# Windowed-attention scores from split queries and keys, saved to DRAM by the projection blocks

## The chip, the cores and the metric

One core of one Trainium2 chip runs the whole program. The metric is the device time of one execution in microseconds (us), the median of several. The core's engines are TensorE (PE, matrix products; its weight loads are listed as PEld), VectorE (DVE), ScalarE (ACT), GpSimd (POOL) and SyncE (SP, which here only issues DMAs). Each works through its own instruction list in order.

## The reference: what is computed

One layer of a hybrid trunk on 1024 tokens of 1024 channels. A normed input is multiplied by `w_in`; the columns go to three groups of heads, the joined outputs are multiplied by `w_out` and added; then follow a gated MLP with a short convolution, a gated per-layer embedding and a last norm. The change touches group B, the mixture of dilated attention windows (4 heads of width 64):

```python
for window, dil in SW_PATTERNS:        # (128, 1), (512, 4), (2048, 16)
    o, lse = banded_causal_attention(stride_gather(q, dil), stride_gather(k, dil),
                                     stride_gather(v, dil), window // dil)
    ...
wts = jax.nn.softmax(jnp.stack(lses, 0), axis=0)
o = jnp.sum(wts[..., None] * jnp.stack(outs, 0), axis=0)
```

The kernel forms it as one masked softmax over all keys up to the query, with the logarithm of how many windows hold a key added to its score. Group A is HGRN2 (4 heads of 128), group C is RWKV-7.

## The kernel before, in words

**Products in two kinds.** Dense products are made from split operands: a value's high part (type fp32r, the cast on line 104 or 152) and the rest (the subtraction on line 106 or 154); high by high, high by rest and rest by high are three fp32r products (`mm3`, lines 122 to 131). Products on raw fp32 operands, the attention scores among them, show as two records in the trace for each product in the program.

**The mixing phase** (`phase_mix`, line 301) has two stages. In the first, `rwkv` alternates the two head pairs of group C with projections of 128 columns, numbered by the list on line 492 and grouped by `FILL` on line 508. A projection block (`project_rest`, line 419) makes 48 products into a PSUM tile `dp`, evicts it on DVE or ACT into an SBUF tile `zst` (two buffers) and stores that to a DRAM tile z*j* on SP's queue (line 433). Blocks 24, 25, 26 are queries, keys and values of the first head pair of group B, 27, 28, 29 those of the second; 8 to 23 are the four blocks (f, q, v, gate) of each HGRN head. The last block made in this stage is 27. Four are left: 28, 29, 19, 23.

In the second stage (line 310) four generators take turns in a list written on lines 318 to 321: A (HGRN heads 0 and 2), B (heads 1 and 3), C (`swa`, the attention), F (`project_late`, the four blocks left, whose PSUM tiles are named `zp`). A scheduler then sets each engine's list from this program. Stream C loads q, k and v of a pair on POOL's queue (`swa_load`, line 1033; four buffers of the tag `sslot`), and for each of 8 blocks of 128 queries makes scores (`swa_scores`, line 1052), adds mask and takes the row extreme (line 1070, DVE), exponentiates (line 1072, ACT), transposes (line 1086) and multiplies by the values (line 1099). The score products on line 1063 use 64 rows of the array for each head. HGRN heads take their tiles from a pool of 11 (`slot`).

**The outputs** of the eight groups of 128 channels stay in SBUF (`self.o`). `o_split` (line 1117) splits one into the operands of the `w_out` product when those operands (`self.O`) exist; until then it notes it in `done`, and the end of `project_late` (lines 465 to 467) splits what is noted. As F's end is reached in the program after all other streams, all eight are noted; the scheduler moves each split to where its operands and buffers are ready. `phase_out` (line 1124) then multiplies: `rows(m)` takes the groups in the order 6, 7, 0, 1, 4, 2, 3, 5, the first two row blocks for both halves of the tokens.

The one-time load of masks, `ctmp` (line 281, POOL's queue), is placed in the pool `pre0` that opens with group C.

Of the kernel before, what the change touches and what calls it, by code (L numbers as in the profile page):

```python
# [18 lines left out]
P = 128  # L19
# [60 lines left out]
class Trunk:  # L80
# [220 lines left out]
    def phase_mix(self):  # L301
        nc, tc = self.nc, self.tc
        self.mix_norm()
# [115 lines left out]
    def project_rest(self, js, hooks={}):  # L419
# [3 lines left out]
        for j in js:  # L423
# [6 lines left out]
            for part in parts:  # L430
                self.finish(kind, *part)
            d = self.zpool.tile([P, T], F32, tag=f"z{j}", name=f"z{j}")
            nc.sync.dma_start(d, t)
            self.z[j] = d

# [9 lines left out]
    def project_late(self, js):  # L445
# [19 lines left out]
        self.O = self.xall()  # L465
        for k in self.done:
            self.o_split(k)

# [16 lines left out]
    def rwkv(self):  # L485
# [194 lines left out]
    def rwkv_norm(self, p, sg, d, hf):  # L680
# [9 lines left out]
        if hf == 0:  # L690
            d["o"] = self.keep.tile([P, T], F32, tag="oc", name=self.nm("oc"), bufs=2)
        o = d["o"][:, sl]
# [19 lines left out]
        if hf:  # L712
            self.o[6 + p] = d["o"]
            self.dump(f"o{6 + p}", d["o"])

    def dump(self, name, t):
# [316 lines left out]
    def swa_load(self, sp, p):  # L1033
        d = {"p": p}
        for i, n in enumerate("qkv"):
            d[n] = self.zload(24 + 3 * p + i, lambda n: sp.tile([P, T], F32, tag="sslot", name=self.nm(n), bufs=4),
                              self.nc.gpsimd)
        return d

    def swa_values_in(self, d):  # L1040
        nc, vc = self.nc, d["v"]
        V = self.sp.tile([P, T], F32, tag="sslot", name=self.nm("sV"), bufs=4)
        for hf in (0, 1):
            pt = self.mxp.tile([P, HT], F32, tag="mx", name=self.nm("vt"))
            for c in range(4):
                nc.tensor.transpose(pt[:, c * P:(c + 1) * P], vc[:, hf * HT + c * P:hf * HT + (c + 1) * P], self.ident)
            nc.scalar.copy(V[:, hf * HT:(hf + 1) * HT], pt)
        d["V"] = V.rearrange("p (b c) -> p b c", c=P)

    HEADS = slice(0, 64), slice(64, 128)  # L1050

    def swa_scores(self, sp, d, qb):
# [7 lines left out]
        for b in range(0, nk, HT):  # L1060
            w = min(HT, nk - b)
            for h, hs in enumerate(self.HEADS):
                nc.tensor.matmul(pq[h][:, b:b + w], d["q"][hs, qb * P:nk], d["k"][hs, b:b + w], start=True, stop=True)
        lgs = []
# [590 lines left out]
```

## Time and profile before

| what | us |
|---|---|
| median of 3 executions | 1521.87 |
| lowest and highest | 1519.84 and 1521.97 |
| the profiled execution | 1520.86 |
| its span, first to last instruction | 1519.0 |
| mean granted TensorE clock in it | 0.986 of full speed |
| PE busy | 1468.0 |
| DVE busy | 1087.5 |
| ACT busy | 634.8 |
| POOL busy | 431.6 |

The profile is one execution. Its times count from the start of the span. A row of its timeline gives start, length, engine, line, operation, output and inputs, and in brackets how long the engine stood idle before it and what ended that. Matmuls overlap in the pipeline, so their lengths add up to more than the time that they take; the distance from start to start is the better price.

### The profile page before, as it was taken

Reading aid. Unit: us, or ns where it says so; the run is one execution under the profiler, and the core shown is the slowest. Engines: PE = TensorE matmul, PEld = TensorE weight load, DVE = VectorE, ACT = ScalarE, POOL = GpSimd, SP = SyncE. Lnnn points to the kernel's source line nnn. Section 1 sums busy time; section 2 is a strip of 40 time slices with the busy share of each in tenths; the row PEclk is TensorE's granted clock in tenths of the full one; section 3 lists DMA queues with packets and bytes.
Section 4 is the critical chain, followed back from the end, with each engine's and each line's share of the span. In section 5 each row is a group of like instructions: output and inputs, shape, how many; then the busy total and the mean of one; then the engine's idle time right before and its main releaser. Section 6 shows DMA issues by size and latency. Waiting matters only on the chain. (4 is left out here: it accounts for less than half of the span.)

```text
span 1519.0 us, 20098 instructions
## 1 busy us (share of the span) xinstructions
PE 1468.0 (97%) x7452; PEld 1213.5 (80%) x7452; DVE 1087.5 (72%) x1574; ACT 634.8 (42%) x1091; POOL 431.6 (28%) x360
## 2 busy tenths in 40 slices
PE   8999999999999899999999999999999999999995
PEld 7888887888877686778778888888888888888774
DVE  7666443674456578745888888888888799767684
ACT  6533322323324545425454444444444444455541
POOL 2234221315222132113124444444444000003330
PEclk9999999999999999999999999999999999999998
DMA  6124002123052121166333333333333873451352
GB/s 216 56 90 125 15 29 84 56 90 84 1 214 64 70 70 56 43 216 200 111 111 104 104 104 104 105 104 105 104 104 109 308 276 99 123 145 52 109 182 75
DMA packets 78865, 167.82 MB, mean 110 GB/s; under 512 B 19952, under 2 KB 20080, under 8 KB 78768
## 3 DMA queue, kind: packets, MB, share of 16 engines
q1 hardware_dynamic: 64992, 145.44, 29.3%
q10 hardware_dynamic: 12688, 17.04, 3.4%
q0 software_dynamic: 1088, 4.06, 0.8%
q8 instruction: 58, 0.95, 0.3%
q14 instruction: 39, 0.32, 0.1%
HBM read 120.12 MB, written 46.40 MB: 110 GB/s over the span
## 5 line engine op out<-in xcount | busy, mean ns | idle before, releaser
L127 PE MATMUL dp<-xh,whi 128*128 128x512 f32 x544 | 185.7, 399 | 1.4 <-ACT xh L367 1.4
L129 PE MATMUL dp<-xl,whi 128*128 128x512 f32 x544 | 182.8, 393 | 0.4 <-DVE xl L368 0.3
L131 PE MATMUL dp<-xh,wlo 128*128 128x512 f32 x544 | 182.0, 393 | 0.5 <-DVE wlo L106 0.5
L106 POOL TENSOR_TENSOR wlo<-wraw,whi 128x512 fp32r<-128x512 f32 x59 | 80.1, 1358 | 270.7 <-ACT whi L104 266.1
L106 POOL TENSOR_TENSOR wlo<-raw,whi 128x512 fp32r<-128x512 f32 x84 | 134.8, 1623 | 76.2 <-ACT whi L104 76.2
L104 ACT CAST whi<-wraw 128x512 fp32r<-128x512 f32 x120 | 73.1, 618 | 167.6 <-PE dp L129 120.4
L1210 PE MATMUL bg<-t,whi 128*128 128x512 f32 x352 | 133.2, 389 | 0.0
L127 PEld LDWEIGHTS dp<-xh,whi 128*128 128x128 f32 x544 | 100.8, 188 | 24.3 <-issue 3.3
L131 PEld LDWEIGHTS dp<-xh,wlo 128*128 128x128 f32 x544 | 101.8, 188 | 22.1 <-DVE wlo L106 1.3
L129 PEld LDWEIGHTS dp<-xl,whi 128*128 128x128 f32 x544 | 101.6, 188 | 22.2 <-DVE xl L368 1.2
L106 POOL TENSOR_TENSOR wlo<-s,whi 128x512 fp32r<-128x512 f32 x44 | 64.2, 1459 | 172.2 <-ACT whi L104 172.2
L1501 PE MATMUL bg<-t,whi 128*128 128x512 f32 x308 | 95.2, 390 | 0.0
L1501 PE MATMUL bv<-t,whi 128*128 128x512 f32 x308 | 94.9, 389 | 0.0
L104 ACT CAST whi<-raw 128x512 fp32r<-128x512 f32 x88 | 52.7, 620 | 94.9 <-issue 48.5
L104 ACT CAST whi<-s 128x512 fp32r<-128x512 f32 x66 | 38.9, 620 | 122.0 <-PE bg L1210 113.3
L106 DVE TENSOR_TENSOR wlo<-wraw,whi 128x512 fp32r<-128x512 f32 x61 | 50.7, 831 | 43.5 <-ACT whi L104 40.1
L1210 PEld LDWEIGHTS bg<-t,whi 128*128 128x128 f32 x352 | 66.1, 188 | 13.8
L168 POOL TENSOR_TENSOR rst<-rst,mhalf 128x4 f32<-128x4 f32 x8 | 9.8, 1226 | 230.6 <-DVE rst L166 230.6
L1501 PEld LDWEIGHTS bv<-t,whi 128*128 128x128 f32 x308 | 57.8, 188 | 12.0
L1501 PEld LDWEIGHTS bg<-t,whi 128*128 128x128 f32 x308 | 57.8, 188 | 11.8
L1210 PE MATMUL bg<-t,wlo 128*128 128x512 f32 x176 | 67.2, 389 | 0.0
L1497 ACT CAST t<-t 128x512 fp32r<-128x512 f32 x77 | 47.8, 622 | 44.4 <-PE bv L1501 30.3
(406 smaller groups left out, 3702.4 us busy)
## 6 DMA issues: line engine op xcount, KB each, us to landing
raw<-in_ffn_up_dram SPq DMA_DIRECT2D x44, 512.0 KB, 3.7
wraw<-in_w_in_dram SPq DMA_DIRECT2D x29, 512.0 KB, 3.7
z<-zst SPq DMA_DIRECT2D x18, 512.0 KB, 3.1
gb<-ct SPq DMA_DIRECT2D x33, 256.0 KB, 2.0
t<-gb SPq DMA_DIRECT2D x33, 256.0 KB, 2.8
t<-gt SPq DMA_DIRECT2D x33, 256.0 KB, 2.7
zl<-z SPq DMA_DIRECT2D x16, 512.0 KB, 3.5
wraw<-in_ple_gate_dram SPq DMA_DIRECT2D x16, 512.0 KB, 3.7
```

The lines of the kernel that those rows point to most:

```text
L104: nc.scalar.copy(hi, src)
L106: eng.tensor_tensor(lo, src, hi.bitcast(F32), ALU.subtract)
L127: nc.tensor.matmul(ps[hf], wh, xh[hf], start=first, stop=False)
L129: nc.tensor.matmul(ps[hf], wh, xl[hf], start=False, stop=False)
L131: nc.tensor.matmul(ps[hf], wl, xh[hf], start=False, stop=last)
L168: nc.gpsimd.tensor_tensor(r2, r, self.mhalf[:, :4], ALU.pow)
L1210: nc.tensor.matmul(ps, w[part == 2][:, s], X[k][part == 1], start=start and k == part == 0, stop=k == 3 and part == 2, skip_group_check=no ...
L1497: nc.scalar.copy(xh, x)
L1501: nc.tensor.matmul(ps[m], wt[part == 2][:, m * P:(m + 1) * P], (xh, xl)[part == 1], start=k == part == 0, stop=k == NK - 1 and part == 2)
```

## The change

The projection blocks 24, 25, 27 and 28 (queries and keys) are evicted as before, then split: an ACT copy makes the fp32r high part `zhi` (another `zst` buffer), a DVE subtraction leaves the rest in place, and both are stored. For each query block four small loads build two stationary tiles `qs`: the high part of one head's queries on its 64 rows, their rest on the other 64. The keys' high part of each head is loaded twice, on both halves of the rows (`kh`), the rest once (`kl`). A score is then one product over 128 rows (high and rest of the queries by the keys' high part) and one over 64 rows (high by rest), both fp32r, where it was one fp32 product over 64 rows.

What goes with it: all loads of the attention are issued on SP's queue; block 27 and 28 trade places with 22, so that 28 is the last block before the second stage and 29, 22, 19, 23 are left; every output is stored to DRAM by `o_split` and loaded again at the end of `project_late`; the outputs of group C move from the pool that lives through the phase to the first stage's pool; HGRN's pool has 10 tiles.

```diff
-        self.O, self.done = None, []
-        for p in (0, 1):
-            self.o_split(6 + p)
...
-            self.slots, self.NSLOT = slots, 11
+            self.slots, self.NSLOT = slots, 10
...
+            if j in (24, 25, 27, 28):
+                hi = self.keep.tile([P, T], F32R, tag="zst", name=self.nm("zhi"), bufs=2)
+                nc.scalar.copy(hi, t)
+                nc.vector.tensor_tensor(t.bitcast(F32R), t, hi.bitcast(F32), ALU.subtract)
+                self.zsave(f"h{j}", hi.bitcast(F32))
+                self.zsave(f"l{j}", t)
+            else:
+                self.zsave(j, t)
...
         for k in self.done:
+            self.o[k] = self.zload(f"o{k}", self.slot)
             self.o_split(k)
...
-        js = iter((*range(8, 16), 24, 25, 26, 16, 17, 18, 20, 21, 22, 27, 28, 29, 19, 23))
+        js = iter((*range(8, 16), 24, 25, 26, 16, 17, 18, 20, 21, 27, 28, 29, 22, 19, 23))
...
+        for h in (0, 1):
+            t = sp.tile([P, T], F32R, tag="kk", name=self.nm("kh"), bufs=5)
+            for q in self.HEADS:
+                nc.sync.dma_start(t[q].bitcast(F32), self.z[f"h{j + 1}"][self.HEADS[h]])
+            d["kh"].append(t)
+        d["kl"] = sp.tile([P, T], F32R, tag="kk", name=self.nm("kl"), bufs=5)
+        nc.sync.dma_start(d["kl"].bitcast(F32), self.z[f"l{j + 1}"])
+        d["qs"] = self.swa_queries(sp, d, 0)
+        d["v"] = self.zload(j + 2, lambda n: sp.tile([P, T], F32, tag="lg", name=self.nm(n), bufs=4))
...
+    def swa_queries(self, sp, d, qb):
+        qs = []
+        for h in (0, 1):
+            t = sp.tile([P, P], F32R, tag="qs", name=self.nm("qs"), bufs=4)
+            for i in (0, 1):
+                self.nc.sync.dma_start(t[self.HEADS[h ^ i]].bitcast(F32), d["z"][i][self.HEADS[h], qb * P:(qb + 1) * P])
+            qs.append(t)
+        return qs
...
+            for h in (0, 1):
+                nc.tensor.matmul(pq[h][:, b:b + w], d["qs"][h], d["kh"][h][:, b:b + w], start=True, stop=False)
             for h, hs in enumerate(self.HEADS):
-                nc.tensor.matmul(pq[h][:, b:b + w], d["q"][hs, qb * P:nk], d["k"][hs, b:b + w], start=True, stop=True)
+                nc.tensor.matmul(pq[h][:, b:b + w], d["qs"][h][hs], d["kl"][hs, b:b + w], start=False, stop=True)
+        if qb < 7:
+            d["qs"] = self.swa_queries(sp, d, qb + 1)
...
     def o_split(self, k):
         if self.O is None:
+            self.zsave(f"o{k}", self.o[k])
             self.done.append(k)
             return
```

The change also reorders each engine's list. On SP, where the second stage begins, stand in the kernel before the load of the last projection weights, the store of block 22, the first four HGRN loads (z8, z9 of head 0; z12, z13 of head 1) and only then the store of the last block, 27:

```order
L95 DMA wraw_855_4423<-in_w_in_dram 128x1024
L433 DMA z22_3522<-zst_660_3519 128x1024
L471 DMA zl_678_3633<-z8_801 128x1024
L471 DMA zl_679_3635<-z9_973 128x1024
L471 DMA zl_749_3904<-z12_1168 128x1024
L471 DMA zl_750_3906<-z13_1236 128x1024
L433 DMA z27_3606<-zst_674_3604 128x1024
```

At the same place of SP's list in the changed kernel stand the rest of block 28's split (zl28; its high part is the row ahead), the keys' rest kl, the four loads of the first query block, the values, and z8 and z9 of HGRN head 0:

```order
L441 DMA zl28_3629<-zst_677_3622 128x1024
L1053 DMA kl_681_3656<-zl25_2092 128x1024
L1063 DMA qs_682_3658<-zh24_1999 64x128
L1063 DMA qs_682_3658<-zl24_2001 64x128
L1063 DMA qs_683_3661<-zh24_1999 64x128
L1063 DMA qs_683_3661<-zl24_2001 64x128
L479 DMA zl_684_3664<-z26_2466 128x1024
L479 DMA zl_685_3666<-z8_801 128x1024
L479 DMA zl_686_3668<-z9_973 128x1024
```

So the first loads of the second stage moved from ahead of the last block's store to behind it. On PE, in the kernel before, products of `phase_out` (dp, operands xh and xl) stand among the last of HGRN head 3 and the attention; these are the first of them:

```order
L1086 MATMUL swt_1020_5151<-cst_76,lg_993_5016 128x128 x4
L127 MATMUL dp_1100_5501<-xh_1089_5403,whi_1098_5497 128x512
L1086 MATMUL swt_1021_5157<-cst_76,lg_993_5016 128x128 x3
L919 MATMUL hsc_1026_5172<-qt_948_4828,ks_1010_5109 128x128 x4
L127 MATMUL dp_1100_5501<-xh_1073_5387,whi_1098_5497 128x512
L129 MATMUL dp_1100_5501<-xl_1090_5404,whi_1098_5497 128x512
```

In the changed kernel the first product of `phase_out` on PE follows the last transposes of HGRN head 3 (vt from ho):

```order
L991 MATMUL hpo_1091_5519<-hV_1080_5463,hS_995_5033 128x128
L1011 MATMUL vt_1097_5548<-cst_76,ho_1090_5518 128x128 x4
L1011 MATMUL vt_1098_5554<-cst_76,ho_1090_5518 128x128 x4
L127 MATMUL dp_1146_5704<-xh_1127_5590,whi_1144_5700 128x512
L127 MATMUL dp_1146_5704<-xh_1111_5574,whi_1144_5700 128x512
L129 MATMUL dp_1146_5704<-xl_1128_5591,whi_1144_5700 128x512
```

The 35 products that stood ahead of those transposes moved behind them.

More of the change, by code (lines that the diff above doesn't have):

```diff
@@ L302, in phase_mix @@
         nc, tc = self.nc, self.tc
+        self.O, self.done = None, []
         self.mix_norm()
@@ L431, in project_rest, with zsave @@
                 self.finish(kind, *part)
-            d = self.zpool.tile([P, T], F32, tag=f"z{j}", name=f"z{j}")
-            nc.sync.dma_start(d, t)
-            self.z[j] = d
+            if j in (24, 25, 27, 28):
[6 more added lines that the diff above has]
+                self.zsave(j, t)
+    def zsave(self, j, t):
+        self.z[j] = self.zpool.tile([P, T], F32, tag=f"z{j}", name=f"z{j}")
+        self.nc.sync.dma_start(self.z[j], t)
     def finish(self, kind, dst, src, r):
@@ L690, in rwkv_norm @@
         if hf == 0:
-            d["o"] = self.keep.tile([P, T], F32, tag="oc", name=self.nm("oc"), bufs=2)
+            d["o"] = self.slots.tile([P, T], F32, tag="oc", name=self.nm("oc"), bufs=2)
         o = d["o"][:, sl]
@@ L714, in rwkv_norm @@
             self.dump(f"o{6 + p}", d["o"])
+            self.o_split(6 + p)
     def dump(self, name, t):
@@ L1033, in swa_load @@
     def swa_load(self, sp, p):
[L1034 to L1037, printed above, removed]
-        return d
+        nc, d = self.nc, {"p": p}
+        j = 24 + 3 * p
+        d["z"] = self.z[f"h{j}"], self.z[f"l{j}"]
+        d["kh"] = []
+        for h in (0, 1):
[7 more added lines that the diff above has]
+        d["v"] = self.zload(j + 2, lambda n: sp.tile([P, T], F32, tag="lg", name=self.nm(n), bufs=4))
+        return d
+    def swa_queries(self, sp, d, qb):
[6 more added lines that the diff above has]
+        return qs
     def swa_values_in(self, d):
         nc, vc = self.nc, d["v"]
-        V = self.sp.tile([P, T], F32, tag="sslot", name=self.nm("sV"), bufs=4)
+        V = self.sp.tile([P, T], F32, tag="sV", name=self.nm("sV"), bufs=1)
         for hf in (0, 1):
```

## The prediction

> **What bounds the kernel now.** I read the page first (busy shares, the span in 40 slices), then busy time by windows, then the timeline around each place that the change touches.
>
> ```profile
> PE 1468.0 (97%) x7452; PEld 1213.5 (80%) x7452; DVE 1087.5 (72%) x1574; ACT 634.8 (42%) x1091; POOL 431.6 (28%) x360
> PE   8999999999999899999999999999999999999995
> DVE  7666443674456578745888888888888799767684
> PEclk9999999999999999999999999999999999999998
> 480.00:520.00 40.00, 40.00 (x255) 31.16 (x256) 24.12 (x44) 19.27 (x36) 6.08 (x5) 1.00 0.08 27
> 520.00:560.00 40.00, 32.92 (x239) 28.15 (x236) 24.62 (x44) 19.65 (x37) 8.43 (x8) 0.87 0.30 106
> 560.00:600.00 40.00, 36.41 (x259) 29.12 (x258) 33.58 (x63) 22.44 (x47) 14.24 (x12) 0.96 0.23 73
> 600.00:620.00 20.00, 18.95 (x153) 14.22 (x152) 18.84 (x40) 12.01 (x24) 3.87 (x3) 1.00 0.08 27
> ```
>
> The last four rows are windows; behind start, end and length stand the busy times of PE, PEld, DVE, ACT and POOL, the granted clock, the DMA share and GB/s. PE sets the pace nearly everywhere. The attention runs from 445 to 644 us. Until 520 PE is never idle; from 520 to 560 it lacks 7 us and runs at 0.87 of its clock; from 560 to 620 DVE is busy 52.4 of 60 us and PE still 55.4. So a microsecond saved on PE counts fully in the first half of this stage and partly in the second, and a wait at the head of PE's list there moves everything behind it.
>
> **The scores themselves.** The timeline of PE gives the price of a burst by the distance to the next row:
>
> ```profile
> 455.00 0.70 PE L1063 MATMUL swq<-zl,zl 64*128 64x256 f32 x4
> 455.63 0.44 PE L1086 MATMUL swt<-cst,lg 128*128 128x128 f32 x2
> 462.80 0.92 PE L1063 MATMUL swq<-zl,zl 64*128 64x384 f32 x4
> 463.64 0.44 PE L1099 MATMUL swo<-pT,sV 128*64 128x128 f32 x4
> 519.52 1.13 PE L1063 MATMUL swq<-zl,zl 64*128 64x512 f32 x4
> 520.58 1.53 PE L1099 MATMUL swo<-pT,sV 128*64 128x128 f32 x24
> 513.88 0.47 PE L127 MATMUL zp<-xh,whi 128*128 128x512 f32 x1
> 519.21 0.39 PE L131 MATMUL zp<-xh,wlo 128*128 128x512 f32 x1
> 453.12 1.95 PE L898 MATMUL hsc<-zl,hk 128*128 128x128 f32 x16
> ```
>
> A burst is two heads by two records. It takes 0.63, 0.84 and 1.06 us for 256, 384 and 512 keys: 0.2 us fixed and 0.21 for each 128 keys. The two heads therefore share the array: the time is that of two records, not four. A burst of 128 keys is then 0.42. The code has 12 bursts of 512 (blocks 3, 4, 5 and 6 once and block 7 twice, for each of two pairs) and 4 each of 384, 256 and 128: 12.7 + 3.4 + 2.5 + 1.7 = 20.3 us, a little more where the heads stand apart.
>
> The fp32r products of a projection follow each other every 0.23 us (the first and last of 24 above, (519.21 - 513.88) / 23). The new burst has two such products over 128 rows and two over 64 rows. If the latter overlap as the old ones do, a burst of 512 costs 3 x 0.23 + 0.2 = 0.89; if not, 1.12. Scaled by width, with 0.12 us as least step of a small product (1.95 / 16), 384, 256 and 128 cost 0.72, 0.56 and 0.56, or 0.89, 0.68 and 0.68. The sum is 18.0 us or 22.4. So what can be gained in products is small: 2.3 us at best by this sum, where heads stand apart before perhaps 5, or a loss of 2. I take a gain of 3, range -2 to 6.
>
> The fixed 0.2 us is weighed once more, since it falls on each change between 128-row and 64-row products, and the new code changes in and out in each of 24 bursts, the old one only in each of 16 blocks. The Trainium skill, "TensorEngine Tiling (Array Packing)", section "Key Properties", says that changing the tiling mode drains TensorE. By that rule the 0.2 us is a price of every change, as counted above; without it the new sum would be 4.8 us lower.
>
> **The start of the stage.** These rows show what PE, DVE and SP did there, and the usual landing times (issues, KB, median us to landing, within 440 to 660 or 40 to 440 us):
>
> ```profile
> 434.89 3.07 SPq L471 DMA_DIRECT2D zl<-z  x4
> 441.13 0.81 DVE L877 TENSOR_SCALAR zl<-zl,olb,lb 128x1024 f32<-128x1024 f32 x1 [5.52 <-DMA zl<-z]
> 443.63 0.62 PE L131 MATMUL dp<-xh,wlo 128*128 128x512 f32 x2
> 445.06 0.48 PE L1063 MATMUL swq<-zl,zl 64*128 64x128 f32 x2
> 446.08 1.22 DVE L438 TENSOR_TENSOR zst<-dp,rstd 128x1024 f32<-128x1024 f32 x1
> zl<-z SPq DMA_DIRECT2D x12, 512.0 KB, 3.3
> z<-zst SPq DMA_DIRECT2D x17, 512.0 KB, 3.1
> At<-scz SPq DMA_DIRECT2D x4, 64.0 KB, 3.1
> L441 ACT ACTIVATE zst<-dp x18: 594/600/1028, 91.7 to 425.7; 128x512 f32<-128x512 f32 x16, 128x1024 f32<-128x1024 f32 x2
> ```
>
> Before, the HGRN loads were issued from 434.9, nine microseconds ahead of the last product of block 27 (443.9), and PE went on with scores at 445.06. In the changed list kl, the first qs, the values, z8 and z9 stand behind both stores of block 28. That block ends on PE at the same 443.9; then DVE evicts (1.2, to 445.3), ACT copies 1024 elements (1.0, to 446.5), DVE subtracts (1.2, to 447.8), SP issues the store, kl and four qs (6 x 0.33, to 449.9), and loads land 3.1 to 3.3 us after their issue: kl at 451.7, the last qs near 452.5, the values at 453.4, z8 and z9 near 454. PE's next rows are the scores, then the transposes of the values, then the products of F, so it waits from 443.9 to about 452.5, where it lost about 1.4 before: 7 us more.
>
> A long wait has a second price, seen at 528 us:
>
> ```profile
> 528.74 0.80 PE L1063 MATMUL swq<-zl,zl 64*128 64x128 f32 x4 [4.01 <-DMA zl<-z]
> 528.70:535.00 6.30, 5.91 (x25) 5.00 (x26) 1.05 (x6) 0.88 (x4) 0.00 (x0) 0.50 0.09 36
> ```
>
> After 4.01 us of idleness PE had half its clock for 6.3 us, which lost about 3 us of work. Eight idle microseconds bring at least that: +3. The start of the stage costs 10 us (range 4 to 14: less if HGRN, whose loads come 13 us late, can catch up; more if the loads, 3 MB with the two stores, queue behind each other).
>
> **The middle.** The same 4.01 us vanish in turn: they were the load of the second pair's queries and keys, which needed the four `sslot` buffers of the first. Now kh has five buffers, its second pair is loaded early, and between the last read of the first kh and the first need of the second kl PE's list holds transposes, HGRN products and 24 products of F, over 6 us against a landing time of 3.3. The gain is 4 us and the 3 of the clock: -7 (range -8 to -3, if another late load takes its place).
>
> **The end of the stage.** The products of `phase_out` that filled PE's waits stand behind HGRN head 3 now:
>
> ```profile
> 627.02 0.48 PE L127 MATMUL dp<-xh,whi 128*128 128x512 f32 x1
> 654.69 0.39 PE L131 MATMUL dp<-xh,wlo 128*128 128x512 f32 x1
> 656.87 1.06 PE L1002 MATMUL vt<-cst,ho 128*128 128x128 f32 x8 [1.79 <-DVE ho L996]
> 657.69 0.48 PE L131 MATMUL dp<-xh,wlo 128*128 128x512 f32 x1
> L152 ACT CAST xh<-zl x8: 620/622/628, 553.7 to 659.0; 128x512 fp32r<-128x512 f32 x8
> L154 POOL TENSOR_TENSOR xl<-zl,xh x4: 1275/1299/1686, 557.5 to 659.0; 128x512 fp32r<-128x512 f32 x4
> ```
>
> They are 35 by 0.23 = 8 us, between the first and second row. About half stood in the wait ahead of 656.87, where HGRN's chain sets the time; their going shortens that chain by perhaps 1 us. So +7 (range 3 to 9). The reloading of the outputs hides: groups 6, 7, 0 and 4 can be split while head 3 ends; 1, 2 and 5 land about 4 us after the store of output 3 is issued; output 3 needs 3.1 + 3.3 and its split 0.6 + 1.3, so some 9 us, and PE has six groups of 12 products, 16 us, to do first. POOL makes a rest each 1.3 us, PE uses up a group each 2.7.
>
> The splits leave the stage, 8 rests on DVE and 16 casts on ACT: where DVE is the busiest (560 to 620) this gives back something, at most 8 x 0.68 = 5 us; I take 2.
>
> **The very beginning.**
>
> ```profile
> 3.00:22.00 19.00, 17.25 (x80) 13.53 (x79) 14.69 (x23) 14.98 (x28) 4.44 (x6) 1.00 1.02 387
> 34.08 0.63 POOL L281 DMA_DIRECT2D ctmp<-in_cst_dram  x1 [7.17 <-DVE rst L166]
> ```
>
> The load of the masks (128 x 1280 fp32, 0.66 MB) was issued at 34 us, when the queues were quiet. The outputs of group C no longer push `pre0` onto memory that is in use, and POOL's list has this load second of all, among loads that already fill the DMA engines at 387 GB/s. 0.66 MB at that rate is 1.7 us of later weights and inputs: +1 (0 to 2).
>
> The four splits cost 4 x 1.0 on ACT and 4 x 1.2 on DVE. For 24, 25 and 27 PE has the next block's 48 products, 11 us, while evicting, splitting and storing take 7, so both `zst` buffers are free in time: nothing. Bared, 2.2 us each; that is block 28, counted above.
>
> **The sum**, on the profiled execution's 1520.86, whose span is 1519.0 and which lies 1.0 below the median: scores -3, start of the stage +10, middle -7, end +7, splits out of the way -2, beginning +1: +6. On the median of 1521.87 that is 1527.9.
>
> **The rivals.** *Faster, the late start is absorbed.* If the second half of the stage is paced by DVE and by its round trips to PE rather than by PE, the late start shrinks to 4 (only PE's products of F come late, and they have no early reader), and relief is the full 5, with the scores' 6: -6 + 4 - 8 + 5 - 5 + 1 = -9, 1513. For it speaks DVE's 18.84 of 20 us after 600; against it that PE is not idle at all from 480 to 520, so nothing there can absorb 10 us. It decides where that stretch shows idle PE now. *Slower still, SP's list.* 68 more small loads go through it, in order, among stores that wait for F's evictions; the loads of a query block (issue 0.33 each, landing 3) stand behind such stores. If each of the 14 blocks after the first of a pair waits 1 us for its qs, that is +14: 1542. Its price decides if any score waits more than a microsecond for a DMA. *The change does not do what it says*: the small fp32r products run no faster than before. That is the upper end of the scores, +2 instead of -3: 1533, inside the range. *It cancels*: a start of 6 and an end of 4 give -1, 1521.
>
> Chances: forecast 0.42, absorbed 0.28, SP's list 0.17, cancels 0.13. A difference of 0.2%, 3 us, is about what a measurement of this kernel can tell. The forecast's own range, 1519 to 1536, lies mostly above 1525. Faster 0.30, same 0.15, slower 0.55. With the rivals the range that should hold 8 in 10 is 1512 to 1541.
>
> **What would show it.** Right: PE idle for 7 to 9 us before the first score with a DMA named, half clock after it; no wait of 4 us in the middle; the first dp product behind the last transposes of ho, without a gap for a split. Wrong: scores that start within 3 us of block 28's end, a new wait for qs or kl later in the stage, PE idle between the products of `phase_out`, or a first stage that ends at another time than about 444 us.

## The result and the profile after

The changed kernel takes 1535.83 us, the median of 4 runs (1534.95 to 1537.42), against 1521.03 for the kernel before on the same chip: a ratio of 1.0099 with a 95% interval of 1.0087 to 1.0111. It is slower by about 15 us, where the forecast was 6. The sign was right; a term of the sum was not.

The page of the changed kernel, busy shares and the granted clock in 40 slices, and two of the windows of the second stage that were shown of before (busy times of PE, PEld, DVE, ACT and POOL, clock, DMA share, GB/s):

```profile
PE 1469.4 (96%) x7452; PEld 1220.4 (80%) x7452; DVE 1092.3 (71%) x1577; ACT 642.0 (42%) x1097; POOL 431.2 (28%) x354
PEclk9999999999989999999999999999999999999998
480.00:520.00 40.00, 39.93 (x271) 32.14 (x270) 26.70 (x54) 18.20 (x35) 6.09 (x5) 0.98 0.27 80
520.00:560.00 40.00, 38.17 (x301) 32.83 (x301) 27.78 (x54) 23.76 (x42) 6.03 (x5) 1.00 0.38 134
```

PE does the same number of products in the same busy time in a longer span (1534.4 against 1519.0), so the loss is waits and clock. The dip of 520 to 560 is gone, as forecast; a new dip of the clock stands in the twelfth slice, where the stage begins.

Three rows cut the span into pieces that can be compared between kernels: the first score, the last transposes of HGRN head 3 (vt from ho), and the spreading of the norm's factor behind `phase_out` (L174). Of the changed kernel:

```profile
454.47 0.45 PE L1090 MATMUL swq<-kh,qs 128*128 128x128 f32 x1 [9.32 <-DMA qs<-zh]
658.79 1.94 PE L1011 MATMUL vt<-cst,ho 128*128 128x128 f32 x8 [7.34 <-DVE ho L1005]
730.55 0.65 PE L174 MATMUL ps_ss<-cst,rst 128*128 128x128 f32 x4 [0.56 <-POOL rst L168]
```

Of the kernel before, the third of them (the other two, 445.06 and 656.87, stand in the prediction):

```profile
713.55 0.65 PE L174 MATMUL ps_ss<-cst,rst 128*128 128x128 f32 x4 [0.57 <-POOL rst L168]
```

The first score comes 9.4 us later. The way from there to the last transposes is 204.3 instead of 211.8, so 7.5 shorter. The tail from there to L174 is 71.8 instead of 56.7, so 15.1 longer. What remains is 803.8 instead of 805.4. The sum is 9.4 - 7.5 + 15.1 - 1.6 = 15.4, the difference of the spans. The table gives the same pieces for all runs, read from the same three rows of each timeline; the labels are those of the experiments below. A ratio compares medians with the kernel before on the same chip, while the pieces come from one profiled execution: that of b_rt took 2.8 us more than its median, that of a_fend 2.6 less.

| kernel | ratio to before (95%) | first score | way | last transposes | tail |
|---|---|---|---|---|---|
| before | 1 | 445.1 | 211.8 | 656.9 | 56.7 |
| changed | 1.0099 (1.0087 to 1.0111) | 454.5 | 204.3 | 658.8 | 71.8 |
| b_rt | 1.0082 (1.0064 to 1.0101) | 444.8 | 212.0 | 656.8 | 71.9 |
| b_sc | 0.9941 (0.9926 to 0.9956) | 444.4 | 203.9 | 648.3 | 56.7 |
| b_mid | 1.0005 (0.9996 to 1.0014) | 450.0 | 206.7 | 656.7 | 56.7 |
| a_fend | 1.0078 (1.0062 to 1.0093) | 456.0 | 207.6 | 663.6 | 60.1 |
| a_pool | 1.0130 (1.0109 to 1.0152) | 456.4 | 203.4 | 659.7 | 71.5 |
| a_o7 | 1.0064 (1.0051 to 1.0076) | 451.8 | 200.0 | 651.8 | 72.1 |
| a_ns9 | 1.0092 (1.0076 to 1.0109) | 455.0 | 201.8 | 656.9 | 72.5 |
| a_start_ns9 | 1.0113 (1.0099 to 1.0127) | 458.6 | 201.0 | 659.6 | 72.0 |
| a_start_kk4 | 1.0134 (1.0118 to 1.0149) | 459.5 | 203.8 | 663.3 | 72.0 |
| a_start_fend | 1.0098 (1.0085 to 1.0112) | 460.2 | 209.8 | 669.9 | 60.8 |
| a_early | 1.0033 (1.0023 to 1.0042) | 448.2 | 198.0 | 646.2 | 71.8 |
| a_early_f29 | 0.9958 (0.9942 to 0.9974) | 447.9 | 201.2 | 649.1 | 56.6 |

### The profile page after: what moved, and what is told of

Its sections match the earlier page's. It is cut to its first block, busy times and chain, and to the rows that moved or that the text cites. A ratio compares the mean times of both kernels' runs of the same rounds, so it can differ in the third digit from the quotient of the medians.

```text
span 1534.4 us, 20277 instructions
## 1 busy us (share of the span) xinstructions
PE 1469.4 (96%) x7452; PEld 1220.4 (80%) x7452; DVE 1092.3 (71%) x1577; ACT 642.0 (42%) x1097; POOL 431.2 (28%) x354
```

## The experiments

Two theories stood at first. E: the end was undersized, because the 35 products of `phase_out` that came behind the chain bring bare waits and half clock with them. S: the late start is carried through, and the end costs no more than its products. They are not exclusive, so each part of the change was done or undone by itself.

### The round trip of the outputs alone (b_rt)

In the kernel before:

```diff
+            self.z[f"o{k}"] = self.zpool.tile([P, T], F32, tag=f"zo{k}", name=f"zo{k}")
+            self.nc.sync.dma_start(self.z[f"o{k}"], self.o[k])
             self.done.append(k)
...
         for k in self.done:
+            self.o[k] = self.zload(f"o{k}", self.slot)
             self.o_split(k)
```

> The kernel before, with one part of the change alone: every output is stored to DRAM and loaded again at the end of project_late. In its PE list no product of phase_out is left ahead of the last transposes of HGRN head 3 (35 in the kernel before). Theory E (the end of the stage is what the forecast undersized): the chain of HGRN head 3 ends about when it did (last transposes at 655 to 657 us), PE waits 5 to 8 us ahead of it instead of 1.8, then 35 products x 0.23 = 8 us come on behind, at half clock for some 4 us of them (+2), and perhaps a wait for weights (+0 to 4): 9 to 14 us slower, 1530 to 1535. Theory S (the late start of the stage is carried through to the end, and the round trip costs only its 8 us less what the chain gains): 3 to 7 us slower, 1524 to 1528. Theory N (the round trip hides): within 2 us of the kernel before.

The ratio is 1.0082, some 12 us. The timeline of PE in this run shows the two rows that bound its tail:

```profile
656.80 1.94 PE L1003 MATMUL vt<-cst,ho 128*128 128x128 f32 x8 [7.34 <-DVE ho L997]
728.71 0.65 PE L174 MATMUL ps_ss<-cst,rst 128*128 128x128 f32 x4 [0.56 <-POOL rst L168]
```

The last transposes come when they did before (656.80 against 656.87): the 35 products had stood in waits of PE and cost the chain nothing. PE now waits 7.34 us there instead of 1.79, and the tail is 15.2 longer, the same as in the changed kernel. That is theory E, and the round trip by itself suffices for the whole of the longer tail.

Where do the 15 come from? Some 35 x 0.23 = 8.1 are the products. The rest shows in the changed kernel's own rows. Two windows of the tail are at half clock:

```profile
655.80:662.50 6.70, 3.71 (x13) 3.35 (x14) 6.13 (x5) 1.78 (x4) 6.70 (x5) 0.50 0.01 4
693.30:696.60 3.30, 2.83 (x7) 1.82 (x6) 0.91 (x1) 0.64 (x2) 2.72 (x2) 0.50 0.39 96
```

And PE waits once for the rest of a split output (0.40 us) and then for the weights of a later row block (first ACT's rows, then PE's):

```profile
691.24 0.63 ACT L193 ACTIVATE sqt<-h 128x512 f32<-128x512 f32 x1 [3.25 <-DVE h L1172]
691.77 2.16 ACT L104 CAST whi<-wraw 128x512 fp32r<-128x512 f32 x4
669.94 0.49 PE L129 MATMUL dp<-xl,whi 128*128 128x512 f32 x1 [0.40 <-POOL xl L154]
692.95 0.54 PE L127 MATMUL dp<-xh,whi 128*128 128x512 f32 x1 [2.84 <-ACT whi L104]
694.39 0.79 PE L131 MATMUL dp<-xh,wlo 128*128 128x512 f32 x1 [0.47 <-POOL wlo L106]
```

The half clock behind the wait of 7.34 us costs half of 3.71, the waits 0.40 and 2.84 + 0.47, the second stretch at half clock half of 2.83. That is 8.1 + 1.9 + 0.4 + 3.3 + 1.4 = 15.1, the whole of it.

Why are the weights late? On ACT's list four casts of them stand behind a square (L193) that itself waits for DVE to add PE's last product, so PE has nothing left to do until they are made. In the kernel before, two of the four stood ahead of that square:

```profile
674.61 1.13 ACT L104 CAST whi<-wraw 128x512 fp32r<-128x512 f32 x2
678.91 0.63 ACT L193 ACTIVATE sqt<-h 128x512 f32<-128x512 f32 x1 [3.18 <-DVE h L1140]
```

Another cause suggests itself: ACT also issues the loads of the residual (h from xT), 12 us later than before (from 671.3 on) and up to 683.7, ahead of those casts. The other runs decide against it. In a_early these loads are issued as early as in the kernel before, and PE waits all the same; in b_mid they take 11.16 us, and PE does not wait (rows of a_early, then of b_mid):

```profile
659.06 7.55 ACTq L1163 DMA_DIRECT2D h<-in_xT_dram  x6
678.62 2.16 ACT L104 CAST whi<-wraw 128x512 fp32r<-128x512 f32 x4
679.79 0.50 PE L127 MATMUL dp<-xh,whi 128*128 128x512 f32 x1 [2.90 <-ACT whi L104]
```

```profile
658.82 11.16 ACTq L1131 DMA_DIRECT2D h<-in_xT_dram  x8
```

In all ten runs of the table with the four casts behind the square PE waits 2.84 to 3.18 us for them; in the four with two or three of them ahead of it (before, b_sc, b_mid, a_early_f29) it waits for weights 0.17 us at most. Why the scheduler sets the list one way or the other is not shown.

### The end of project_late earlier in the list of turns (a_fend)

In the changed kernel:

```diff
-                order += "C" * (r in self.TURNS) + "A" + "B" * (r > 5) + "F" * (r % 2 and r < 16)
+                order += "C" * (r in self.TURNS) + "A" + "B" * (r > 5) + "F" * (r % 2 and r < 18)
```

> The changed kernel with the end of project_late two rounds later in the list of turns than its last block instead of behind all other streams (turns of F up to round 17): the outputs that are done by then are loaded and split there, the rest are split straight from SBUF, and 40 products of phase_out stand ahead of the last transposes of HGRN head 3 again. Theory E: the end gives back its 10 to 14 us, and 1522 to 1526 is left, with the late start still in it. Theory S: the chain's end is set by the late start, so at most 4 us come back: 1532 to 1536. Against both: the split operands take PE, DVE and ACT time inside the stage again (up to 5 us), so 1527 to 1531 would leave E with the smaller part.

The ratio is 1.0078, some 3 us less than the changed kernel's, with intervals that overlap a little. The tail falls from 71.8 to 60.1: with products of `phase_out` ahead of the transposes again, 11.7 us of the 15.1 go. The 3.4 that stay are in the main the wait for weights (2.84 + 0.24), since the four casts still stand behind the square. But the way grows by 3.3. The timeline of all engines around the end of head 1 shows what came in between:

```profile
584.10 1.14 ACT L152 CAST xh<-zl 128x512 fp32r<-128x512 f32 x2 [0.54 <-DMA zl<-zo]
589.86 0.78 DVE L154 TENSOR_TENSOR xl<-zl,xh 128x512 fp32r<-128x512 f32 x1
591.67 1.64 POOL L1003 TENSOR_TENSOR hrs<-hss,mhalf 128x8 f32<-128x8 f32 x1
```

The casts and rests of the outputs that came back early stand on ACT and DVE among the last steps of head 1, ahead of its factor (hrs), and PE waits 8.91 us for its transposes (at 594.71), where the changed kernel waited 4.24. That the splits cause this longer wait is argued from their place in the lists. So the place of the end seems to matter as much as that it is early.

### The pair's loads on POOL's queue (a_pool)

In the changed kernel, and in the same way for kl, the values and the first qs of a pair:

```diff
-                nc.sync.dma_start(t[q].bitcast(F32), self.z[f"h{j + 1}"][self.HEADS[h]])
+                nc.gpsimd.dma_start(t[q].bitcast(F32), self.z[f"h{j + 1}"][self.HEADS[h]])
```

> The changed kernel with the loads of a pair (kh, kl, the first qs, the values) issued on POOL's queue, as before the change, the later qs still on SP's. On SP's list the loads of HGRN head 0 then stand ahead of the stores of block 28. Theory S: PE's wait at the start of the stage falls from 9.3 us to 4 or less and the half clock behind it goes, and all 8 to 10 us reach the end: 1526 to 1528. Theory E: the chain of HGRN and DVE work takes the late start up before the end of the stage, so only 1 to 4 us come back: 1532 to 1535. In both the last transposes of head 3 tell it: 649 to 651 us in S, 655 to 658 in E, against 658.8 in the changed kernel.

Neither came: the wait grew to 10.90 us, the first score came at 456.4, and the ratio is 1.0130. This does not clear SP's list. In the changed kernel the list does what the prediction said: the loads of the first queries (qs) are issued right behind the store of the rest of block 28, and PE's wait ends when they land.

```profile
448.78 0.33 SPq L441 DMA_DIRECT2D zl<-zst  x1
449.65 0.52 SPq L1063 DMA_DIRECT2D qs<-zh  x1
451.49 0.60 SPq L1063 DMA_DIRECT2D qs<-zl  x1
```

On POOL's queue that gate is gone, but two others stand there: the keys wait for the store of output 7, and the last of the first queries for the landing of the keys.

```profile
442.52 2.18 POOL L1050 DMA_DIRECT2D kh<-zh  x4 [11.50 <-DMA zo<-oc]
450.70 0.52 POOL L1063 DMA_DIRECT2D qs<-zl  x1 [3.74 <-DMA kh<-zh]
```

The loads also land later, kl 10.7 us behind its issue where it was 4.8. The windows of the changed kernel and of the kernel before from 436 to 456 us show how full the queues are:

```profile
436.00:456.00 20.00, 10.68 (x45) 8.39 (x43) 5.41 (x8) 3.88 (x6) 1.73 (x2) 0.79 0.95 307
```

```profile
436.00:456.00 20.00, 18.62 (x96) 15.06 (x95) 11.73 (x25) 5.26 (x10) 3.59 (x5) 1.00 0.62 237
```

In the changed kernel the DMA engines are busy for 95% of these 20 us and move 307 x 20 = 6.1 MB; before it was 62% and 4.7 MB. Stores of split blocks, keys loaded twice, an output stored and the masks of the attention (0.5 MB, issued at 441.7 where it was 417.6) come together there. The rate is low besides: from 446 to 451 us the engines are fully busy at 294 GB/s, where they moved 415 from 437 to 442 in the kernel before. Whether the loads of 64 rows each (kh) slow them was not tried by itself.

### The new products alone (b_sc)

In the kernel before (the tiles of queries and keys are of type fp32r besides; no rests are formed, so the scores are not the reference's):

```diff
+            for h in (0, 1):
+                nc.tensor.matmul(pq[h][:, b:b + w], d["q"][:, qb * P:nk], d["k"][:, b:b + w], start=True, stop=False)
             for h, hs in enumerate(self.HEADS):
-                nc.tensor.matmul(pq[h][:, b:b + w], d["q"][hs, qb * P:nk], d["k"][hs, b:b + w], start=True, stop=True)
+                nc.tensor.matmul(pq[h][:, b:b + w], d["q"][hs, qb * P:nk], d["k"][hs, b:b + w], start=False, stop=True)
```

> The kernel before with the new products of the scores and nothing else: queries and keys are loaded as one piece each, bit for bit as fp32r, and each score is one product over 128 rows and one over 64 rows in place of one fp32 product. The 128-row product adds both heads and no rest is formed, so the scores are not the reference's. Between the two profiles PE's own work of the stage fell by 5 us (idle time and lost clock taken off). If PE paces the stage: 3 to 5 us faster, 1516 to 1518. If the chain through DVE paces it: 0 to 2 us faster, 1519 to 1521. If the change in and out of 64-row products costs what the old bursts saved: no gain or up to 2 slower.

It is 9 us faster (0.9941), more than any of the three cases. The wait of 4 us in the middle is gone here too, although its buffers are those of before. POOL's timeline shows the load of the second pair's keys, in this run and in the kernel before:

```profile
511.88 0.59 POOL L1037 DMA_DIRECT2D k<-z  x1 [8.91 <-PE swq L1066]
```

```profile
521.31 1.12 POOL L471 DMA_DIRECT2D zl<-z  x2
```

The scheduler put the last scores of the first pair ahead of 24 products of F, where they had stood behind, so the buffers came free 9.4 us earlier. How much of the 9 is the products themselves is told by single bursts. In the changed kernel, PE's timeline has one burst of 512 keys with the heads apart (four rows from 519.54) and one with them together (the two rows from 521.43):

```profile
519.54 0.47 PE L1090 MATMUL swq<-kh,qs 128*128 128x512 f32 x1
519.94 0.50 PE L1092 MATMUL swq<-kl,qs 64*128 64x512 f32 x1
520.37 0.50 PE L1090 MATMUL swq<-kh,qs 128*128 128x512 f32 x1
520.80 0.50 PE L1092 MATMUL swq<-kl,qs 64*128 64x512 f32 x1
521.23 0.44 PE L1117 MATMUL swt<-cst,lg 128*128 128x128 f32 x2
521.43 0.71 PE L1090 MATMUL swq<-kh,qs 128*128 128x512 f32 x2
522.07 0.50 PE L1092 MATMUL swq<-kl,qs 64*128 64x512 f32 x2
522.50 1.09 PE L951 MATMUL vt<-cst,zl 128*128 128x128 f32 x8
```

In the kernel before, one head alone, and the next row:

```profile
506.10 1.12 PE L1063 MATMUL swq<-zl,zl 64*128 64x512 f32 x2
507.15 0.44 PE L1086 MATMUL swt<-cst,lg 128*128 128x128 f32 x2
```

Together, the burst takes 522.50 - 521.43 = 1.07 us to the next row, as before (1.06). Apart, a head takes 0.85 instead of 1.05. The step into the burst is not in these distances: an old burst starts with a product of 64 rows, and the product ahead of it takes longer for that. An estimate from the traces takes in both: over all bursts of the stage, from the start of the product ahead to the start of the product behind, less the usual step of the one ahead and all idle time (stretches at half clock are in it), the scores take 31.0 us in the kernel before, 27.4 in b_sc and 26.5 in the changed kernel. So the products save about 4 us. The rest of the 9 of b_sc comes with its list; no run parts it further.

### What sets the start: output 7, the tenth tile, the stores (a_o7, a_start_ns9, a_start_kk4, a_ns9, a_early)

Output 7 back in the pool that lives through the phase, paid for with a tile of HGRN's pool:

```diff
-            self.slots, self.NSLOT = slots, 10
+            self.slots, self.NSLOT = slots, 9
...
-            d["o"] = self.slots.tile([P, T], F32, tag="oc", name=self.nm("oc"), bufs=2)
+            d["o"] = (self.keep if p else self.slots).tile([P, T], F32, tag="oc", name=self.nm("oc"), bufs=1)
```

> The changed kernel with output 7 in the pool that lives through the phase, as before the change, so that no tile of the second stage lies on its memory and waits for its store; HGRN's pool has 9 tiles in place of 10 to make room. Theory G (the store of output 7 gates the loads of the second stage: the first of them, kh, is issued at 441.7 us in the changed kernel, behind a wait for it): kh and kl are issued by 439, PE's wait ahead of the first score falls from 9.3 us to 6 to 7 (what is left is qs behind the stores of block 28), the time falls by 2 to 4, to 1532 to 1534. Theory Q (the loads behind block 28 alone set the start): no change, 1535 to 1537.

The ratio is 1.0064: 5 us better than the changed kernel, more than theory G had. SP's timeline, first of the changed kernel, then of this run:

```profile
438.10 0.32 SPq L441 DMA_DIRECT2D zo<-oc  x1
441.68 2.39 SPq L1050 DMA_DIRECT2D kh<-zh  x4
```

```profile
437.28 0.32 SPq L441 DMA_DIRECT2D zo<-oc  x1
437.76 3.42 SPq L1050 DMA_DIRECT2D kh<-zh  x4
```

The keys had waited for the store of output 7 to land, since a tile of the new stage lies on its memory. Without that they are issued 3.9 us earlier. The first score comes 2.6 earlier; 0.8 of both is an execution whose first stage ends earlier, and PE's wait falls from 9.32 to 7.48 us, a little less than theory G had. The control, 9 tiles and nothing else:

> The changed kernel with 9 tiles in HGRN's pool in place of 10 and nothing else: the control for the run that kept output 7. If the tile itself moves the chain (in both runs with 9 tiles the time from the first score to the last transposes of head 3 was 200 to 201 us, in four with 10 tiles 203 to 204), the time is 2 to 4 lower than the changed kernel's, 1531.5 to 1534, with the wait at the start unchanged at 9 to 10 us. If the whole gain came from output 7, it is 1535 to 1537.

1.0092, with the wait at the start unchanged (9.22 us): the tile shortens the way by 2.5 us in the trace, but the time cannot be told from the changed kernel's. Output 7 carries most of the gain.

Then blocks 27 and 28 one place earlier, so that 21 is the last, and the pair's loads on POOL's queue as in a_pool; a_start_kk4 is the same with the room made among the keys' buffers (four for kh and kl, 10 tiles for HGRN):

```diff
-        js = iter((*range(8, 16), 24, 25, 26, 16, 17, 18, 20, 21, 27, 28, 29, 22, 19, 23))
+        js = iter((*range(8, 16), 24, 25, 26, 16, 17, 18, 20, 27, 28, 21, 29, 22, 19, 23))
```

> Output 7 kept as in the run before (9 tiles), the loads of a pair on POOL's queue, and block 28 two places earlier in the list (21 is the last block before the second stage), so that no store of the split stands ahead of the stage's first loads. Theory S (the late start is carried through to the end of the stage): PE's wait ahead of the first score falls below 4 us, the last transposes of HGRN head 3 come at 649 to 652 us in place of 658.8, and the time is 1525 to 1529. Theory A (the chain through DVE absorbs it): the wait falls too, but the last transposes come at 656 or later and the time is 1533 to 1536. If the loads themselves fill the queues (3.5 MB at some 390 GB/s are 9 us) the wait stays over 6 us and neither is told.

> The same with room made in another place: HGRN's 10 tiles stay, and kh and kl have four buffers in place of five, so that the second pair's keys wait for the first pair's last score. Theory S: the start as in the run before, and in the middle a wait of 2 to 4 us for kh or kl with half clock behind it, so 1528 to 1533. If it is faster than with 9 tiles, HGRN's tenth tile is worth more than the fifth buffer.

Both misses: 1.0113 and 1.0134, with waits of 11.22 and 11.51 us. The loads no longer stand behind a store of the split (in a_start_ns9 the keys go out from 440.1, the first queries from 442.8), but they take 9 to 15 us to land (medians of kh, qs and kl), with the DMA engines fully busy at 241 GB/s from 446 to 451 us: the loads themselves fill the queues, as the last sentence of the first expectation allowed. The runs tell two things. Four buffers for the keys bring no wait in the middle, so the fifth was not what removed it. And most of a late start reaches the end of the way: a_start_kk4 starts 5.0 us later than the changed kernel and ends 4.5 later, a_start_ns9 starts 3.5 later than a_ns9 and ends 2.7 later.

So blocks 27 and 28 were made long before, on top of a_o7. This moves the bytes of their stores, and in SP's list the first queries no longer stand behind them.

```diff
-        js = iter((*range(8, 16), 24, 25, 26, 16, 17, 18, 20, 21, 27, 28, 29, 22, 19, 23))
+        js = iter((*range(8, 16), 24, 25, 26, 27, 28, 16, 17, 18, 20, 21, 29, 22, 19, 23))
```

> The run that kept output 7 (9 tiles), and blocks 27 and 28 made right behind 24 to 26, long before the second stage, so that their four stores (2 MB) and their split are gone from the place where the second stage begins; the last blocks before it are 20 and 21. In SP's list kh, kl, qs and the values then stand ahead of the last store. Theory S with the queues full (the wait is the time of some 6 MB at 300 GB/s): PE's wait ahead of the first score falls from 7.5 to 2 to 4 us, every microsecond of it reaches the end, last transposes at 646 to 648 us (651.8 with output 7 kept), time 1525 to 1527. Theory A (absorbed): the wait falls, the last transposes stay at 650 to 652, 1529 to 1531.

```profile
448.18 0.30 PE L1090 MATMUL swq<-kh,qs 128*128 128x128 f32 x1 [3.31 <-DMA qs<-zl]
```

The wait falls to 3.31 us and the ratio to 1.0033. The first queries are issued from 441.5 on, some 8 us earlier than in the changed kernel; how much of the gain is their place in the list and how much the bytes is not parted. Against a_o7 the first score comes 3.6 us earlier and the last transposes 5.6; the stretch at half clock behind the wait is shorter too (a granted clock of 0.78 from 451 to 456 us, where it was 0.50). Theory S holds: what the start loses, the end of the stage shows.

### Start and end together (a_start_fend, a_early_f29)

The earlier end on the slow start (a_start_kk4 with the line of a_fend):

> The run before (four buffers) with the end of project_late at round 17 as well, so that 35 to 40 products of phase_out stand ahead of the last transposes of HGRN head 3. In the changed kernel that edit alone brought 4 to 6 us. If start and end add up: 1522 to 1527, about the kernel before. If the splits that come back into the stage meet a fuller DVE: no gain over the run before.

1.0098, 5 us below a_start_kk4: again some 11 us less tail and 6 us more way. And on top of a_early, with the end of `project_late` at a round that keeps the splits behind the factors of heads 0 to 2:

```diff
-                order += "C" * (r in self.TURNS) + "A" + "B" * (r > 5) + "F" * (r % 2 and r < 16)
+                order += "C" * (r in self.TURNS) + "A" + "B" * (r > 5) + "F" * (r % 2 and r < 16 or r == 29)
```

> The run before, and the end of project_late at round 29 of the list of turns: outputs 6, 7, 0, 4, 1 and 2 are loaded again and split while head 3 still runs, 5 and 3 are split straight from SBUF, and 35 products of phase_out stand ahead of the last transposes again; POOL's rests stand behind the factors of heads 0 to 2. Theory E: it gives back most of the end (8 for the products, 3 for the clock, 3 for the weights, less 2 to 5 for the splits in the stage): 6 to 11 below the run before, 1515 to 1521, so as fast as the kernel before or faster. If the splits in the stage push the chain out by as much: no gain.

```profile
649.09 1.06 PE L1011 MATMUL vt<-cst,ho 128*128 128x128 f32 x8 [1.76 <-DVE ho L1005]
```

1513.24 us, a ratio of 0.9958 to the kernel before: faster than both kernels. The gain over a_early is 12 us, a little more than expected. The tail is back at 56.6: the products stand in the waits again, the clock holds, and two casts stand ahead of the square again, so that the wait for weights is gone too. In a_fend and a_start_fend, with the products ahead but all casts behind, the tail was 60.1 and 60.8; so some 11 to 12 of the 15 us go with the products and 3 to 4 with the order of ACT's list. The way is 3.2 us longer than in a_early. The ratios of this kernel and of the changed one, 0.9958 and 1.0099, lie 21 us apart, with the same products of the scores in both: the difference is where transfers, splits and products stand.

### A fifth buffer in the kernel before (b_mid)

```diff
-            self.slots, self.NSLOT = slots, 11
+            self.slots, self.NSLOT = slots, 10
...
-            d[n] = self.zload(24 + 3 * p + i, lambda n: sp.tile([P, T], F32, tag="sslot", name=self.nm(n), bufs=4),
+            d[n] = self.zload(24 + 3 * p + i, lambda n: sp.tile([P, T], F32, tag="sslot", name=self.nm(n), bufs=5),
...
-        V = self.sp.tile([P, T], F32, tag="sslot", name=self.nm("sV"), bufs=4)
+        V = self.sp.tile([P, T], F32, tag="sslot", name=self.nm("sV"), bufs=5)
```

> The kernel before with a fifth buffer for queries, keys and values (and 10 tiles for HGRN in place of 11, to make room), so that the second pair's keys are loaded before the first pair's last scores are made, and the wait of 4 us in the middle of the stage goes without any new product. It parts the 8.3 us by which the new products alone shortened the way from the first score to the last transposes of head 3 (211.8 to 203.9 us), where the wait had gone too. As the prediction sized it (middle 7, scores 3): 1513.5 to 1516. If the wait was idle time that the chain through DVE would have spent anyway, and the products carry the gain: 1518 to 1521.

The time does not move (1.0005, 0.9996 to 1.0014), and the run does not part the terms. The wait in the middle is gone and the way is 5.1 us shorter, but this stage began 5 us later, behind a wait for DVE:

```profile
448.15 1.94 PE L1046 MATMUL vt<-cst,zl 128*128 128x128 f32 x8 [4.55 <-DVE hT L929]
```

In the kernel before, the wait in the middle swallows a late start: b_rt came to it 2.1 us later (528.62 - 1.76 = 526.86 against 528.74 - 4.01 = 524.73) and left it at the same time.

```profile
528.62 0.80 PE L1064 MATMUL swq<-zl,zl 64*128 64x128 f32 x4 [1.76 <-DMA zl<-z]
```

So how the shorter way of b_sc (7.9 us) divides stays open. The 4 us estimated for the products and the 4 us of the wait would add up to it.

## Why the prediction was wrong

The direction was right; one term of the sum failed. In the prediction's terms the measured sum is 0.9 + 11.7 - 10.7 + 15.1 - 1.6 = 15.4 where it had 1 + 10 - 12 + 7 = 6.

- **The end of the stage: +7 (range 3 to 9); measured 15.1.** This is the step that failed. The 35 products were counted rightly, 8 us, but three things beside them were not. "Their going shortens that chain by perhaps 1 us": it did not (656.80 in b_rt). The wait of 7.3 us that they left bare has the second price that the prediction itself had named for the start, half clock behind it (1.9 us), and the sum did not charge it here. And "the reloading of the outputs hides" looked at the splits alone, where a gap of only 0.40 us came. The price of 3.3 us and 1.4 of half clock behind it came from the new order of ACT's list, with all four casts of weights behind a square; no term of the sum was for that.
- **The start: +10, with +1 for the beginning; measured 11.7 and 0.9.** The first score comes 9.4 later, 0.9 of it from the beginning, and the products behind it ran at half clock, which costs half of 6.37 us more:

```profile
447.60:461.10 13.50, 6.37 (x19) 5.23 (x20) 4.62 (x10) 4.04 (x8) 0.00 (x0) 0.50 0.84 278
```

  Right in size, and right in its first cause: the wait of 9.32 us with half clock behind it stands where it was forecast, and the first queries go out behind block 28's stores. The steps were sized too small: block 28's rest is stored at 448.8 in place of 447.8, an issue takes 0.6 in place of 0.33 us, and the first score comes at 454.5 in place of 452.5. What the prediction did not see are the full queues and the memory under output 7, which decide once the loads no longer stand behind the stores (a_pool, a_o7, a_start_ns9, a_start_kk4).
- **The middle, the scores and the splits: -7, -3 and -2; measured together -10.7** (the way's -7.5 less the 3.2 of half clock just counted). The wait in the middle is gone, as forecast:

```profile
523.89 0.33 PE L1090 MATMUL swq<-kh,qs 128*128 128x128 f32 x1 [0.30 <-DVE sden L1101]
```

  The reason given, five buffers, is not needed (a_start_kk4). For a new burst the prediction had 0.89 us if the 64-row halves overlap and 1.12 if not; measured is 1.07. They do overlap: two of them take 522.50 - 522.07 = 0.43 us, one alone 520.37 - 519.94 = 0.43. But the change between 128 and 64 rows is paid on the way in (0.64 us for the two products over 128 rows in place of 0.46) and on the way out (0.43 in place of 0.23), and the sum of 0.89 had it once, although the text counts both. So 1.12 came near for another reason. That the -3 agrees with the estimate of 4 us is in part luck: the two sums behind it gave a gain of 2.3 and a loss of 2. Nothing shows the 2 us for the splits.
- **The beginning: +1.** The last product of the last block starts at 444.54, 0.9 us later. The delay is there early: PE's first product with `lora` starts at 51.2 to 51.7 us in before, b_rt, b_sc and b_mid, and at 51.8 to 53.4 in six runs with the changed first stage. That it is the load of the masks is not shown.
- **The rivals.** That the late start is absorbed is refuted by a_start_kk4 and a_early, and from 480 to 520 us, where this rival was to show idle PE, PE is busy 39.93 of 40 us. SP's list with 68 more loads cost nothing later in the stage: PE's groups between 440 and 660 us show no wait for qs but the first one (behind the bar: busy us, mean ns, idle us and what ended it).

```profile
L1090 PE MATMUL swq<-kh,qs 128*128 128x128 f32 x8 | 2.4, 344 | 9.6 <-DMA qs<-zh 9.3 <-DVE sden L1101 0.3
```

  That the new products run no faster is not so: 26.5 us in place of 31.0 by the estimate above.
- **Not foreseen: -1.6 in the rest.** Before, one stretch behind `phase_out` ran at half clock, which the changed kernel has not:

```profile
746.80:750.10 3.30, 3.30 (x11) 2.62 (x10) 2.89 (x5) 0.00 (x0) 0.00 (x0) 0.50 0.31 125
```

## What to carry to other kernels

Work of the next phase that stands inside a chain's waits is free there and dear behind it: count not only its products but the bare wait and the clock behind it. Where a stage begins, look at both: behind which stores its first loads stand in the list, and how many bytes are in flight when they go out. Making the stored blocks earlier mended both and helped; issuing the loads from another queue did not. And a new order of a scheduler's list can be worth more than the operation that caused it. Before naming the cause of such a wait, look for a run that has the cause without the wait, or the wait without the cause.

## What the runs showed of the hardware

**The clock can fall behind short waits too.** In the changed kernel PE waited 1.31 us at 477.7, and the next window is at half clock, with PE busy throughout:

```profile
477.71 1.69 PE L928 MATMUL hsc<-qt,ks 128*128 128x128 f32 x8 [1.31 <-DVE zst L445]
```

```profile
478.30:481.60 3.30, 3.30 (x13) 2.21 (x12) 2.20 (x5) 1.95 (x6) 0.00 (x0) 0.50 0.32 112
```

The Trainium skill, "TensorE: Matmul & The Clock Gate", section "Why this matters for your kernels", advises against idle gaps of more than about 3 us because one idle window brings the clock back to half; this trace has the half clock behind a gap of 1.31 us. Not every such gap does it: behind 1.38 us of idleness that ended at 447.35 in the kernel before, the granted clock stayed at 1.00.

**Two 64-row products on the two halves run side by side, and a change from 64 to 128 rows costs about 0.2 us.** In the rows of the bursts above, one 64-row product of 512 columns takes 520.37 - 519.94 = 0.43 us to the next product over 128 rows, and two on different halves take 522.50 - 522.07 = 0.43. For 384, 256 and 128 columns two take 0.38, 0.32 and 0.25: 0.2 us fixed and 0.06 for each 128 columns. Products over 128 rows follow each other every 0.23 us at 512 columns, which is 0.06 for each 128 and nothing fixed. This agrees with the Trainium skill, "TensorEngine Tiling (Array Packing)", section "Key Properties", by which a change of tiling mode drains TensorE.
